# First weight tile of w1 behind w2, and the parts of Strassen's chunk, begun at other places modulo 256 bytes

## The chip, the cores and the metric

The kernel runs on one core of a Trainium2 chip. Its work lies on five engines with queues of their own: TensorE (PE in the profile, with its weight loads as PEld), VectorE (DVE), ScalarE (ACT), GpSimd (POOL) and SyncE (SP), which here issues the loads from memory. The metric is the time of one execution on the device in microseconds. Two executions of the kernel before took 2197.57 and 2195.24 us, median 2196.4 us.

## The reference

A model of two layers on 256 tokens of 2048 numbers, all in float32: stick-breaking attention, a perceptron, native sparse attention, a perceptron. What the change touches is the perceptron, which runs once per layer:

```python
def sqrelu_mlp(h, w1, w2):
    return jnp.square(jax.nn.relu(h @ w1)) @ w2      # w1: 2048 x 8192, w2: 8192 x 2048

def reference(x, ...):
    h = x
    for layer in range(DEPTH):                       # DEPTH = 2
        ...                                          # h = h + attention(rms_norm(h, ...))
        h = h + sqrelu_mlp(rms_norm(h, mlp_norm_g[layer]), mlp_w1[layer], mlp_w2[layer])
    return h
```

## The kernel before

**Precision.** Every product is made of three: each operand is split into a high part that TensorE's fast float32 form (fp32r) holds exactly and a low part that is the rest, and hi·hi, hi·lo and lo·hi are added up in PSUM. `split` (L129 to L136) makes the parts of a weight chunk: ScalarE writes `hi` (L133), VectorE writes `lo` (L135).

**Chunks.** Weights come in chunks of 512 KB, a tile of 128 partitions by 1024 numbers (4 KB a partition), and each chunk is worked off by one of three functions:

- `chunk_T` (L177) is for w1 (and for q and k). The weight chunk is TensorE's stationary operand, and x (`xs`, high and low) streams past it, 256 columns at a time. A chunk is 24 matmuls (L185): 16 with `hi`, then 8 with `lo`. Every matmul loads other weights.
- `chunk_N` (L151) is for w2 and others. The activations `yhi`, `ylo` are stationary, and the weight chunk streams, 512 columns at a time: 8 matmuls with `hi`, then 4 with `lo` (L155).
- `chunk_S` (L211) is for a quarter of w2: Strassen's seven products in place of eight. The activations (`yhi`, `ylo`, and their sums `ss`) are stationary. What streams, 256 columns at a time, are four tiles: `shi` and `slo` (three quarters of the chunk itself; L221 to L227) and `thi` and `tlo` (four sums of quarters, from `split`, L228). Seven products of three matmuls are 21 matmuls a chunk (L246): 6 stream `shi`, 3 stream `slo`, 8 stream `thi`, 4 stream `tlo`.

**The order of the work.** A perceptron (`mlp`, L390) is done in four groups, `fg` 0 to 3. In each, `group1` (L400) makes 2048 of the 8192 hidden numbers: four calls of `proj_T` (one for each `fb`), each eight chunks of w1, so 32 chunks or 768 matmuls in a row. Then `group2` (L426) takes these through w2: 24 chunks with `chunk_N`, and 8 with `chunk_S` spread among them by a short rule (L430 to L434). So with two perceptrons there are eight groups, 64 calls of `chunk_S`, and six stretches of w1 that directly follow matmuls of w2 (`fg` 1 to 3 of either layer). The stretch of `fg` 0 follows the attention's output projection, and transposes of h stand between its first chunks (L303, from `make_x`). Engines are kept in step by semaphores that the framework sets; their order is that of the code.

**Places.** The tiles `hi` and `lo` of `split`, `shi` and `slo` are 64 numbers (256 bytes) longer than what they hold, and what they hold begins at an offset, in numbers of 4 bytes:

```python
PAD = 64
NEAR, FAR, SUM = 0, 16, 48
```

`chunk_N` uses NEAR (0 bytes), `chunk_T` FAR (64 bytes), `chunk_S` SUM (192 bytes) for all four parts. In the built program the tiles `xs`, `yhi`, `ylo`, `ss`, `shi`, `slo` and every buffer of `hi` and `lo` begin at the same place modulo 256 bytes, and each matmul's slice of them lies a multiple of 256 bytes further on, so the offset alone says how the stationary and the streaming operand of a matmul lie to each other modulo 256 bytes: equal in `chunk_N`, stationary 64 bytes further in `chunk_T`, streaming 192 bytes further in `chunk_S`, which modulo 256 is again stationary 64 bytes further.

Of the kernel before, what the change touches and what calls it, by code (L numbers as in the profile page):

```python
# [9 lines left out]
F32R = mybir.dt.float32r  # L10
# [5 lines left out]
P = 128  # L16
T = 256
NT = T // P
D = 2048
KD = D // P  # L20
NB = 512
# [4 lines left out]
KC = 2  # L26
# [13 lines left out]
def hybrid_kernel(  # L40
# [13 lines left out]
    wsum = None  # L54
# [63 lines left out]
    def drain():  # L118
        while beside:
            for _ in beside.pop(0)[0]:  # L120
                pass

    PAD = 64
    NEAR, FAR, SUM = 0, 16, 48

    def split(raw, o=(NEAR, NEAR)):  # L129
        n = KC * NB  # L130
# [46 lines left out]
    def chunk_T(ps, src, k0, n0, first, last, nk=KC, o=None):  # L177

        nm = KC * NB // P // nk
        hi, lo = src if isinstance(src, tuple) else load_split(src, k0, nk, n0, nm * P, o=o or (FAR, FAR))  # L180
        tiles = [(kk, m) for kk in range(nk) for m in range(nm)]

        def mm(w, x, kk, m, s, e):
            o = ps[m // 2][:, (m % 2) * T:(m % 2 + 1) * T]
            nc.tensor.matmul(o, w[:, kk, m * P:(m + 1) * P], x[:, k0 + kk, :], start=s, stop=e, skip_group_check=True)  # L185

        for kk, m in tiles:
            mm(hi, xhi, kk, m, first and kk == 0 and m % 2 == 0, False)
            mm(hi, xlo, kk, m, False, False)
        pump()  # L190
        for kk, m in tiles:
            mm(lo, xhi, kk, m, False, last and kk == nk - 1)
        pump()

    def proj_T(ps, src, n0, nk=KC, o=None):
        for k0 in range(0, KD, nk):
            chunk_T(ps, src, k0, n0, k0 == 0, k0 + nk == KD, nk, o)

    def proj_Th(src, n0):

# [10 lines left out]
    def chunk_S(ps, src, k0, n0, first, last, ahi, alo, shi, slo, koff=0):  # L211


        W = NB // 2
        raw = load(src, k0, KC, n0, NB)
        flat = raw.rearrange("p k n -> p (k n)")

        ts = wsum.tile([P, 4, W], F32, tag="ts", name="ts")
        b12 = flat[:, 3 * W:].unsqueeze(1).to_broadcast([P, 2, W])
        nc.vector.tensor_tensor(ts[:, :2, :], flat[:, W:3 * W].rearrange("p (a n) -> p a n", a=2), b12, op=OP.subtract)  # L220
        hi, lo = [  # L221
            wsum.tile([P, 3 * W + PAD], F32R, tag=n, name=n, bufs=1)[:, SUM:SUM + 3 * W] for n in ("shi", "slo")
        ]
        nc.scalar.activation(hi, flat[:, :3 * W], AF.Copy)
        nc.vector.tensor_tensor(ts[:, 2, :], ts[:, 0, :], flat[:, 2 * W:3 * W], op=OP.add)
        nc.vector.tensor_tensor(ts[:, 3, :], flat[:, :W], ts[:, 2, :], op=OP.subtract)  # L226
        nc.vector.tensor_tensor(lo, flat[:, :3 * W], hi.bitcast(F32), op=OP.subtract)  # L227
        thi, tlo = split(ts, (SUM, SUM))  # L228
        k = k0 - koff
        y = lambda a, kk, t: a[:, k + kk, t * P:(t + 1) * P]  # L230
        s = lambda a, i: a[:, k // KC, i, :]
        b = lambda w, i: w[:, i * W:(i + 1) * W]
        trivial = [
            (0, y(ahi, 1, 0), y(alo, 1, 0), b(hi, 2), b(lo, 2)),
            (1, y(ahi, 0, 0), y(alo, 0, 0), b(hi, 0), b(lo, 0)),
            (2, s(shi, 3), s(slo, 3), b(hi, 1), b(lo, 1)),
        ]
        sums = [
            (6, s(shi, 2), s(slo, 2), thi[:, 0, :], tlo[:, 0, :]),
            (4, s(shi, 0), s(slo, 0), thi[:, 1, :], tlo[:, 1, :]),  # L240
            (5, s(shi, 1), s(slo, 1), thi[:, 2, :], tlo[:, 2, :]),
            (3, y(ahi, 0, 1), y(alo, 0, 1), thi[:, 3, :], tlo[:, 3, :]),
        ]

        def mm(i, a, w, s, e):
            nc.tensor.matmul(ps[i], a, w, start=s, stop=e, skip_group_check=True)  # L246

        for i, xh, xl, wh, wl in trivial + sums:

            mm(i, xh, wh, first and i in (0, 1, 6, 4), False)  # L250
            mm(i, xl, wh, False, False)
        pump()
        for i, xh, xl, wh, wl in trivial + sums:
            mm(i, xh, wl, False, last)
        pump()
# [134 lines left out]
    def mlp(l, layer, junk, done, last=None):  # L390
        w1, w2 = mlp_w1[l], mlp_w2[l]
        ss = junk.tile([P, 2, KD // 2, 4, P], F32R, name="ss", bufs=1)
        row = junk.tile([P, T], F32, name="row", bufs=1)

        def rows():
            yield
            pb = bcast_rows(make_rstd(layer))
            nc.scalar.activation(row, pb[:, :T], AF.Copy)

        def group1(fg, pools):  # L400

            for fb in range(D // NB):
                ps = [bank(*pools[fb % 2]) for _ in range(NB // P // 2)]
                proj_T(ps, w1, fg * D + fb * NB)
                k, n = fb * (NB // P), NB // P
                a = junk.tile([P, n, T], F32, tag="pre", name="pre", bufs=1)
                for j in range(0, n, 2):
                    nc.vector.scalar_tensor_tensor(
                        a[:, j:j + 2, :], ps[j // 2].rearrange("p (m t) -> p m t", m=2), 0.0,
                        row.unsqueeze(1).to_broadcast([P, 2, T]), op0=OP.max, op1=OP.mult,  # L410
                    )
                s = junk.tile([P, n, T], F32, tag="sq", name="sq", bufs=1)
                nc.scalar.activation(s, a, AF.Square)
                nc.scalar.activation(yhi[:, k:k + n, :], s, AF.Copy)
                nc.vector.tensor_tensor(ylo[:, k:k + n, :], s, yhi[:, k:k + n, :].bitcast(F32), op=OP.subtract)

                sv = s.rearrange("p (j kk) t -> p j kk t", kk=2)
                a1, a2 = [[sv[:, :, kk, t * P:(t + 1) * P] for kk in (1, 0)] for t in range(NT)]
                q = junk.tile([P, 2, 4, P], F32, tag="sums", name="sums", bufs=1)
                nc.vector.scalar_tensor_tensor(q[:, :, 0, :], a2[0], -1.0, a2[1], op0=OP.mult, op1=OP.subtract)  # L420
                nc.vector.tensor_tensor(q[:, :, 2, :], a1[0], a2[0], op=OP.subtract)
                nc.vector.tensor_tensor(q[:, :, 1, :], a2[1], q[:, :, 2, :], op=OP.subtract)
                nc.vector.tensor_tensor(q[:, :, 3, :], a1[1], q[:, :, 1, :], op=OP.subtract)
                split_evac(ss[:, 0, k // 2:k // 2 + 2], ss[:, 1, k // 2:k // 2 + 2], q)

        def group2(fg, plain, strassen, end):  # L426

            NK = KD // KC
            order, si = [], 0
            for i in range(3 * NK):  # L430
                order.append(((0, 1, 3)[i // NK], i % NK))
                if si < NK and i >= (3 + 1.75 * si if end else 4 + 2.25 * si):
                    order.append((2, si))
                    si += 1  # L434
            for nb, i in order:
                k0 = fg * KD + i * KC
                args = (w2, k0, nb * NB, i == 0, i == NK - 1, yhi, ylo)
                if nb == 2:
                    if i == 0:
                        bs, s = banks_S(*strassen)  # L440
                    chunk_S(s, *args, ss[:, 0], ss[:, 1], koff=fg * KD)
                    if i == NK - 1:
                        add_S(nb, bs, s, junk)
                        if end:
                            for n in range(3):
                                done(n, strassen)
                    continue
                if i == 0:
                    ps = [bank(*plain) for _ in range(NT)]
                out = last is not None and end and nb == 3  # L450
                chunk_N(ps, w2, k0, nb * NB, i == 0, i == NK - (2 if out else 1), yhi, ylo, koff=fg * KD,
                        by_token=out and i == NK - 1)
                if i == NK - 1:
                    if out:
                        add_out(nb, ps, last)
                        return
                    add_h(nb, ps)
                    if end and nb == 3:
                        done(nb, plain)

        spawn(rows(), 1)
        A, B = (acc, "acc"), (att, "att")
        for fg in range(DFF // D):
            end = fg == DFF // D - 1
            group1(fg, ((A, B), (B, A))[fg % 2])
            group2(fg, *((A, B), (B, A))[fg % 2], end)
# [200 lines left out]
    with tc.tile_pool(name="m0p", bufs=2) as mp:  # L667
        wsum = mp
# [9 lines left out]
    with tc.tile_pool(name="nsa", bufs=2) as ap, ExitStack() as last:  # L678
# [255 lines left out]
        for i in range(2):  # L934
            cT = cp.tile([P, G, T], F32, tag="cT", name="cT", bufs=1)
            for b in range(2):
                ps = proj_Th(w_in, C0 + i * NB + b * T)
# [61 lines left out]
        for g in range(G):  # L999
            ps = [bank(acc, "acc") for _ in range(NT)]  # L1000
# [16 lines left out]
            ps = proj_N(w_in, g * NB)  # L1017
# [8 lines left out]
    with tc.tile_pool(name="m1p", bufs=2) as mp:  # L1026
        wsum = mp
# [36 lines left out]
```

## Time and profile before

| | |
|---|---|
| median of 2 runs | 2196.4 us (2195.24 to 2197.57) |
| the profiled execution, its time | 2196.84 us |
| its span from first to last instruction | 2195.1 us |
| granted clock of TensorE | 0.999 |
| TensorE busy | 2186.2 us, 14482 matmuls |
| weight loads busy | 1997.6 us |
| VectorE, ScalarE, GpSimd busy | 1484.1, 1164.7, 42.5 us |
| matmuls of w1 and the like (L185) | 8040 |
| matmuls of Strassen's chunks (L246) | 1344 |

The profile is of one execution, taken by the hardware profiler. It says of each engine how long it was busy, what it waited for, and in the timeline when each group of like instructions began. A matmul's length in it is modelled and overlaps that of the next, so the pace of a row of matmuls is read from starts: the start of the next row less that of this one, over the count.

### The profile page before, as it was taken

The page shows a single profiled execution, that of the slowest core. Times are in us where ns is not written, and L with a number is a line of the kernel's source. Part 1 is how long each engine was busy: PE and PEld are TensorE (multiplying, and loading weights), DVE is VectorE, ACT ScalarE, POOL GpSimd, SP SyncE. Part 2 cuts the span into 40 slices and gives each one's busy share as a digit, 9 for nine tenths or more (in the row PEclk, how much of TensorE's full clock was granted, in tenths as well). Part 3 has the DMA queues.
Part 4 walks back from the last instruction along what each step waited for, and adds up shares of the span by engine and source line. Part 5 has one row for each costly group of instructions (what it writes and reads, how often), then busy time and mean ns, then how long its engine had stood idle before and what let it go on. Part 6 is the DMA issues. An engine that isn't in the chain of part 4 may idle for free.

```text
span 2195.1 us, 36040 instructions
## 1 busy us (share of the span) xinstructions
PE 2186.2 (100%) x14482; PEld 1997.6 (91%) x14482; DVE 1484.1 (68%) x1968; ACT 1164.7 (53%) x1537; POOL 42.5 (2%) x75
## 2 busy tenths in 40 slices
PE   9999999999999999999999999999999999999999
PEld 9999988998998998899898888889989989989998
DVE  4655556677667667767777877755776676677676
ACT  5555565455445454445546666655544454554453
POOL 0000000000000000000000011000000000000000
PEclk9999999999999999999999999999999999999999
DMA  6655555665665765665667554456657656656654
GB/s 222 204 180 172 156 182 176 186 197 186 200 190 175 215 187 178 215 185 184 203 182 222 163 144 139 139 164 186 190 189 206 182 192 202 191 183 205 189 186 160
DMA packets 260784, 406.28 MB, mean 185 GB/s; under 512 B 13188, under 2 KB 91912, under 8 KB 260616
## 3 DMA queue, kind: packets, MB, share of 16 engines
q1 hardware_dynamic: 259800, 403.52, 60.0%
q8 instruction: 113, 1.85, 0.3%
q10 hardware_dynamic: 816, 0.46, 0.1%
q14 instruction: 55, 0.45, 0.1%
HBM read 401.83 MB, written 2.10 MB: 184 GB/s over the span
## 4 chain that ended last, share of the span: by engine, by line
PE 99%; DVE 0%; POOL 0%; ACT 0%; issue 0%; DVEq 0%; ACTq 0%; POOLq 0%
PE acc L155 31%; PE acc L185 26%; PE att L185 16%; PE att L155 13%; PE acc L246 4%; PE att L246 4%; PE att L896 1%; PE att L303 1%; PE att L888 0%; PE att L889 0%; PE att L890 0%; PE att L583 0%; PE att L631 0%; PE att L842 0%; PE att L844 0%; PE att L843 0%
## 5 line engine op out<-in xcount | busy, mean ns | idle before, releaser
L133 ACT ACTIVATE hi<-raw 128x1024 fp32r<-128x1024 f32 x687 | 726.5, 1059 | 740.3 <-PE acc L155 227.1
L135 DVE TENSOR_TENSOR lo<-raw,hi 128x1024 fp32r<-128x1024 f32 x687 | 836.0, 1221 | 395.6 <-ACT hi L133 374.7
L185 PE MATMUL acc<-xs,hi 128*128 128x256 f32 x3312 | 420.4, 280 | 1.9 <-ACT hi L133 1.9
L185 PEld LDWEIGHTS acc<-xs,hi 128*128 128x128 f32 x3312 | 400.1, 189 | 2.7 <-ACT hi L133 2.1
L185 PE MATMUL att<-xs,hi 128*128 128x256 f32 x2048 | 259.8, 280 | 0.0
L155 PE MATMUL acc<-hi,yhi 128*128 128x512 f32 x640 | 250.7, 392 | 0.0
L155 PE MATMUL acc<-hi,ylo 128*128 128x512 f32 x640 | 249.3, 390 | 0.0
L185 PEld LDWEIGHTS att<-xs,hi 128*128 128x128 f32 x2048 | 248.3, 189 | 0.3
L185 PE MATMUL acc<-xs,lo 128*128 128x256 f32 x1656 | 226.5, 279 | 0.0
L185 PEld LDWEIGHTS acc<-xs,lo 128*128 128x128 f32 x1656 | 207.4, 189 | 0.0
L155 PE MATMUL acc<-hi,xs 128*128 128x512 f32 x704 | 177.2, 392 | 0.0
L155 PE MATMUL acc<-lo,yhi 128*128 128x512 f32 x640 | 172.4, 390 | 0.0
L155 PEld LDWEIGHTS acc<-hi,xs 128*128 128x128 f32 x704 | 130.3, 188 | 26.6
L155 PE MATMUL att<-hi,yhi 128*128 128x512 f32 x380 | 148.2, 390 | 0.0
L155 PE MATMUL att<-hi,ylo 128*128 128x512 f32 x380 | 147.9, 389 | 0.0
L155 PEld LDWEIGHTS acc<-lo,yhi 128*128 128x128 f32 x640 | 119.5, 188 | 24.9 <-issue 0.4
L155 PEld LDWEIGHTS acc<-hi,ylo 128*128 128x128 f32 x640 | 120.2, 188 | 23.3 <-DVE ylo L290 0.2
L155 PEld LDWEIGHTS acc<-hi,yhi 128*128 128x128 f32 x640 | 120.2, 188 | 23.3 <-ACT yhi L289 0.2
L185 PE MATMUL att<-xs,lo 128*128 128x256 f32 x1024 | 140.4, 280 | 0.0
L185 PEld LDWEIGHTS att<-xs,lo 128*128 128x128 f32 x1024 | 128.7, 189 | 0.0
L220 DVE TENSOR_TENSOR ts<-raw 128x512 f32<-128x512 f32 x64 | 44.3, 692 | 115.6 <-DMA raw<-in_mlp_w_dram 115.5
L133 ACT ACTIVATE hi<-ts 128x1024 fp32r<-128x1024 f32 x64 | 67.8, 1059 | 87.8 <-DVE ts L226 41.8
(290 smaller groups left out, 2501.3 us busy)
## 6 DMA issues: line engine op xcount, KB each, us to landing
raw<-in_mlp_w_dram SPq DMA_DIRECT2D x512, 512.0 KB, 3.9
raw<-in_sb_w_qkv_dram SPq DMA_DIRECT2D x95, 512.0 KB, 3.8
raw<-in_nsa_w_in_dram SPq DMA_DIRECT2D x50, 512.0 KB, 3.8
raw<-in_sb_w_out_dram SPq DMA_DIRECT2D x32, 512.0 KB, 3.9
raw<-in_nsa_w_in_dram SPq DMA_DIRECT2D x64, 256.0 KB, 3.4
raw<-in_nsa_w_out_dram SPq DMA_DIRECT2D x32, 512.0 KB, 3.7
w1t<-in_nsa_cmp_w_dram SPq DMA_DIRECT2D x8, 512.0 KB, 4.9
h<-in_x_dram SPq DMA_DIRECT2D x8, 256.0 KB, 4.1
```

Source lines behind the costliest of these rows:

```text
L133: nc.scalar.activation(hi, raw, AF.Copy)
L135: nc.vector.tensor_tensor(lo, raw, hi.bitcast(F32), op=OP.subtract)
L155: mm = lambda a, b, k, t, s, e: nc.tensor.matmul(ps[t], a[:, k, t * P:(t + 1) * P], b, start=s, stop=e)
L185: nc.tensor.matmul(o, w[:, kk, m * P:(m + 1) * P], x[:, k0 + kk, :], start=s, stop=e, skip_group_check=True)
L220: nc.vector.tensor_tensor(ts[:, :2, :], flat[:, W:3 * W].rearrange("p (a n) -> p a n", a=2), b12, op=OP.subtract)
L246: nc.tensor.matmul(ps[i], a, w, start=s, stop=e, skip_group_check=True)
L303: nc.tensor.transpose(ps[:, j * T + t * P:j * T + (t + 1) * P], h[:, t, (kp + j) * P:(kp + j + 1) * P], ident)
L896: nc.tensor.transpose(ptp[:w, j * P:(j + 1) * P], src(j), ident)
```

## The change

Only places change. The first chunk of w1 of `fg` 1, 2 and 3 in either layer (`fb` 0, `k0` 0) begins 32 bytes into its tiles (`TURN`) where it began 64 bytes in; the other 31 chunks of the stretch stay at 64. In `chunk_S` a counter of the calls picks, for each of the eight groups, another set of four offsets, for `shi` (A), `slo` (B), `thi` (C) and `tlo` (E). In bytes, where all were 192:

| group | shi | slo | thi | tlo | matmuls of a chunk's 21 that stream from another place |
|---|---|---|---|---|---|
| layer 0, fg 0 | 224 | 192 | 192 | 192 | 6 |
| layer 0, fg 1 | 224 | 192 | 192 | 224 | 10 |
| layer 0, fg 2 | 224 | 224 | 192 | 192 | 9 |
| layer 0, fg 3 | 32 | 192 | 192 | 192 | 6 |
| layer 1, fg 0 | 192 | 192 | 224 | 192 | 8 |
| layer 1, fg 1 | 240 | 192 | 192 | 192 | 6 |
| layer 1, fg 2 | 128 | 192 | 192 | 192 | 6 |
| layer 1, fg 3 | 192 | 224 | 192 | 224 | 7 |

No tile changes its size or its place in memory. No instruction is added, taken out or moved: on every engine the two programs have the same instructions in the same order, with the same shapes and waits. Of the matmuls, 144 load their weights from another place (six chunks of 24), and 464 stream from another place (58 in the table, times eight chunks in a group).

```diff
     PAD = 64
-    NEAR, FAR, SUM = 0, 16, 48
+    NEAR, FAR, TURN, SUM = 0, 16, 8, 48
...
-    def proj_T(ps, src, n0, nk=KC, o=None):
+    def proj_T(ps, src, n0, nk=KC, turn=False):
         for k0 in range(0, KD, nk):
-            chunk_T(ps, src, k0, n0, k0 == 0, k0 + nk == KD, nk, o)
+            o = TURN if turn and k0 == 0 else FAR
+            chunk_T(ps, src, k0, n0, k0 == 0, k0 + nk == KD, nk, (o, o))
...
+        A, B, C, E = ((56, 48, 48, 48), (56, 48, 48, 56), (56, 56, 48, 48), (8, 48, 48, 48), (48, 48, 56, 48),
+                      (60, 48, 48, 48), (32, 48, 48, 48), (48, 56, 48, 56))[trial[0] // 8]
+        trial[0] += 1
         hi, lo = [
-            wsum.tile([P, 3 * W + PAD], F32R, tag=n, name=n, bufs=1)[:, SUM:SUM + 3 * W] for n in ("shi", "slo")
+            wsum.tile([P, 3 * W + PAD], F32R, tag=n, name=n, bufs=1)[:, o:o + 3 * W]
+            for n, o in (("shi", A), ("slo", B))
         ]
...
-        thi, tlo = split(ts, (SUM, SUM))
+        thi, tlo = split(ts, (C, E))
...
-                proj_T(ps, w1, fg * D + fb * NB)
+                proj_T(ps, w1, fg * D + fb * NB, turn=fg > 0 and fb == 0)
```

## Rows read from the trace of the kernel before

**Rows 1.** The page: the span, each engine's busy time, and the chain of work that ended last by engine.

```profile
span 2195.1 us, 36040 instructions
PE 2186.2 (100%) x14482; PEld 1997.6 (91%) x14482; DVE 1484.1 (68%) x1968; ACT 1164.7 (53%) x1537; POOL 42.5 (2%) x75
...
PE 99%; DVE 0%; POOL 0%; ACT 0%; issue 0%; DVEq 0%; ACTq 0%; POOLq 0%
```

**Rows 2.** All waits of TensorE for another engine over the whole span: us in total, times, longest.

```profile
PE acc L185 <- ACT hi L133: 1.9, 1, 1.9
PE att L489 <- POOL ident masks.py:199: 1.6, 1, 1.6
PE att L761 <- DVE hs L757: 0.9, 1, 0.9
PE att L796 <- DVE kc L792: 0.5, 1, 0.5
PE acc L508 <- ACT hi L501: 0.2, 1, 0.2
```

**Rows 3.** Busy time by stretch, of the matmuls of L185 alone. The stretches are w1's of `fg` 0 (first and fifth row, from the second chunk behind the last transposes on) and of `fg` 1 to 3 (the others, whole), layer 0 and then layer 1. Columns: stretch, its length, TensorE busy and count, weight loads busy and count, granted clock, share of the DMA engines busy, GB/s.

```profile
415.79:486.51 70.72, 70.72 (x626) 70.68 (x624) 1.00 0.66 193
571.60:662.05 90.45, 90.45 (x768) 90.41 (x767) 1.00 0.65 190
747.15:837.60 90.45, 90.45 (x768) 90.41 (x767) 1.00 0.65 190
922.69:1013.15 90.46, 90.46 (x768) 90.41 (x767) 1.00 0.64 187
1508.51:1579.23 70.72, 70.72 (x626) 70.69 (x624) 1.00 0.65 194
1664.33:1754.78 90.45, 90.45 (x768) 90.41 (x767) 1.00 0.66 190
1839.87:1930.32 90.45, 90.45 (x768) 90.41 (x767) 1.00 0.65 190
2015.42:2105.87 90.45, 90.45 (x768) 90.41 (x767) 1.00 0.65 189
```

**Rows 4.** TensorE's timeline at the last transposes ahead of w1 of `fg` 0, layer 0: start, length in us, engine, line, operands, count.

```profile
412.82 0.38 PE L352 MATMUL att<-ident,rstd 128*128 128x128 f32 x2
412.96 2.09 PE L185 MATMUL acc<-xs,hi 128*128 128x256 f32 x16
414.88 1.07 PE L185 MATMUL acc<-xs,lo 128*128 128x256 f32 x8
415.79 1.98 PE L185 MATMUL acc<-xs,hi 128*128 128x256 f32 x16
```

**Rows 5.** TensorE's timeline at the step from w2 of `fg` 0 to w1 of `fg` 1, layer 0; columns as in rows 4.

```profile
568.88 0.39 PE L155 MATMUL acc<-hi,yhi 128*128 128x512 f32 x1
...
570.69 1.07 PE L155 MATMUL acc<-lo,yhi 128*128 128x512 f32 x4
571.60 2.05 PE L185 MATMUL att<-xs,hi 128*128 128x256 f32 x16
573.48 1.11 PE L185 MATMUL att<-xs,lo 128*128 128x256 f32 x8
574.43 2.05 PE L185 MATMUL att<-xs,hi 128*128 128x256 f32 x16
```

**Rows 6.** TensorE's timeline from the first matmul of Strassen's first chunk (500.13) to the first behind it (502.61), and over the two chunks of `chunk_N` that follow.

```profile
500.13 0.28 PE L246 MATMUL att<-shi,yhi 128*128 128x256 f32 x1
...
502.49 0.28 PE L246 MATMUL att<-lo,yhi 128*128 128x256 f32 x1
502.61 0.39 PE L155 MATMUL acc<-hi,yhi 128*128 128x512 f32 x1
...
505.33 0.39 PE L155 MATMUL acc<-hi,yhi 128*128 128x512 f32 x1
...
508.05 0.39 PE L155 MATMUL acc<-hi,yhi 128*128 128x512 f32 x1
```

**Rows 7.** The costliest groups of the page: how many chunks go through `chunk_S` (L220 is its first instruction on VectorE), and ScalarE's writing of `hi` with its idle time.

```profile
L133 ACT ACTIVATE hi<-raw 128x1024 fp32r<-128x1024 f32 x687 | 726.5, 1059 | 740.3 <-PE acc L155 227.1
...
L220 DVE TENSOR_TENSOR ts<-raw 128x512 f32<-128x512 f32 x64 | 44.3, 692 | 115.6 <-DMA raw<-in_mlp_w_dram 115.5
```

**Rows 8.** TensorE's timeline in native sparse attention's compression, where L750 runs 32 matmuls of 256 columns whose stationary operand (120 columns) begins 224 bytes further, modulo 256, from one matmul to the next.

```profile
1199.17 3.94 PE L750 MATMUL att<-ws,bs 128*120 128x256 f32 x32
1202.95 1.32 PE L155 MATMUL acc<-hi,xs 128*128 128x512 f32 x5
```

**Rows 9.** TensorE's timeline at the step from w1 to w2 of `fg` 1, layer 0: the first two chunks of `chunk_N`.

```profile
662.05 0.40 PE L155 MATMUL att<-hi,yhi 128*128 128x512 f32 x1
662.29 0.40 PE L155 MATMUL att<-hi,ylo 128*128 128x512 f32 x1
662.52 0.39 PE L155 MATMUL att<-hi,yhi 128*128 128x512 f32 x1
...
664.80 0.39 PE L155 MATMUL att<-hi,yhi 128*128 128x512 f32 x1
...
666.61 1.07 PE L155 MATMUL att<-lo,yhi 128*128 128x512 f32 x4
```

More of the change, by code (lines that the diff above doesn't have):

```diff
@@ L121, in drain @@
                 pass
+    trial = [0]
     PAD = 64
-    NEAR, FAR, SUM = 0, 16, 48
+    NEAR, FAR, TURN, SUM = 0, 16, 8, 48
     def split(raw, o=(NEAR, NEAR)):
```

## The prediction

> **What bounds the kernel now.** I read the page first. TensorE is busy for 2186.2 of 2195.1 us, and the chain of work that ended last is TensorE's own for 99% [rows 1]. The view of its waits shows five waits, 5.1 us together; the rest of the span is matmuls one behind the other [rows 2]. So time comes and goes only through the pace at which matmuls follow each other, and the next view to read is the pace by stretch. It shows something odd. The 624 matmuls of w1 of `fg` 0 take 70.72 us, 113.33 ns each; the 768 of each later stretch take 90.45 us, 117.77 ns each. That is the same instruction with the same shape, the same offsets and the same granted clock of 1.00 (2.4 GHz), beside as many bytes a second. Each pace holds from one end of its stretch to the other, through every change of chunk and bank, in both layers [rows 3]. It is not starvation: with a wait for an operand the profile would show TensorE idle, and there is none here. So there are two steady states, and which one holds is settled where the stretch begins.
>
> The timelines show how they begin. In `fg` 0 a pair of transposes breaks the stream, the 24 matmuls behind it take 2.83 us (117.9 ns each), and from the next chunk on the fast pace holds [rows 4, 3]. In `fg` 1 to 3 w1 follows `chunk_N`, whose twelve matmuls take 2.72 us, 226.7 ns each, which is twice 113.33; there w1 starts without a break, at 2.83 us a chunk at once, and stays so [rows 5, 3]. Strassen's chunk, too, follows `chunk_N` without a break: 2.48 us for 21 matmuls, 118 ns each, and `chunk_N` behind it is back at 2.72 us with its first chunk [rows 6]. I take from this that a stream of weights and a stream of moving data step through memory in a fixed rhythm to each other, that the fast rhythm and the slow one both keep themselves up, and that a break or a shift can move one into the other. That is an inference; the rows show only the two paces and where they begin.
>
> **The change part by part.** No instruction comes or goes, so the sum holds paces only. It is made against the profiled execution's 2196.8 us (its span is 2195.1); the median, 2196.4, is 0.4 less.
>
> *The turned chunk of w1.* Six chunks load their weights 32 bytes earlier. What matters is whether the shift in and the shift back leave the rest of the stretch in the slow rhythm or in the fast one. The trace of before has no such shift, so the two bounds are the two paces. If it stays slow, the gain is nothing. If it turns, 744 matmuls behind the first chunk gain 4.44 ns in each of six stretches: 6 x 744 x 4.44 = 19.8 us. For the turned chunk itself I take the price of the settling chunk of `fg` 0, 2.83 us [rows 4], what such a chunk costs now [rows 5], so it is worth nothing. The shift back costs at most what a step between kinds of matmul costs, 0.03 us: `chunk_N` behind w1 takes 2.75 us in place of 2.72 before it is in pace [rows 9, 6]. Six of them are 0.2 us. Nothing else has to speed up: `fg` 0 runs at the fast pace with no wait of TensorE, at 193 GB/s against 187 to 190 [rows 2, 3], and ScalarE, which writes `hi`, has 740 us of idle time ahead of those very instructions [rows 7]; were that cover gone, TensorE would wait for `hi` and the 19.8 us would shrink. I take 19.6 us of gain, since the fast rhythm, once there, outlives everything in its stretch, and one break sufficed to find it; against it stands that all six starts from `chunk_N` go wrong in one and the same way.
>
> *Strassen's parts.* 64 chunks [rows 7] of 21 matmuls, of which 464 stream from another place. Below, the bound is the fast pace for all 1344: (118 - 113.33) x 1344 = 6.3 us of gain. Above, the dearest pace that the rows show outside a break is `chunk_N`'s first two matmuls behind w1, 0.47 us for the two [rows 9] against 0.453 in pace, 8 ns more each: 1344 x 8 = 10.8 us, and 0.03 us at each of the 128 ends, 3.8 us; together 14.6 us of loss. The nearest row is L750's: the same width, with the stationary operand's place running through eight different ones modulo 256 bytes, 3.78 us for 32 matmuls, 118.1 ns each [rows 8]. So a matmul at any of these places costs on average what Strassen's cost now, and I take nothing for the matmuls themselves. But today's chunk hands the stream back in pace, and one at other places has no reason to: 64 x 0.03 = 1.9 us of loss, which I take. Writing to other places costs nothing that counts, since ScalarE and VectorE are 53% and 68% busy [rows 1].
>
> The sum: 2196.8 - 19.6 + 1.9 = 2179.1, so 2179 us.
>
> **The rivals.**
>
> *The shift does nothing to w1.* The slow rhythm may simply follow the weights by 32 bytes and back. For it speaks that it survives 31 changes of chunk in each stretch [rows 3], each of which could have upset it, and that L750's matmuls at ever other places average 118.1 ns, the slow pace and not the fast one [rows 8]. Against it: none of those changes of chunk moves the place modulo 256 bytes, and this one does. Time: 2196.8 + 1.9 = 2198.7 us.
>
> The Trainium skill has a rule that would end in the same place. "TensorE: Matmul & The Clock Gate", section "Step-by-step: what each phase is for", gives TensorE two independent read ports into SBUF, one for the moving operand and one for weight loads, and "SBUF — State Buffer", section "SBUF: two separate sides", says that TensorE never waits on anyone there. By that rule the place of an operand would be worth nothing anywhere, Strassen's parts included, and the time would stay at 2196.8 us. The two paces of one and the same instruction in this trace [rows 3] do not fit it well, but they do not show a place at work either.
>
> *Only some of the stretches turn.* Each stretch follows another layout of Strassen's chunk, so the six need not begin alike. Against it: `chunk_N` finds its pace within a chunk [rows 9] and runs several chunks before w1 begins. With three of six, 2196.8 - 9.8 + 1.9 = 2189 us.
>
> *Strassen's chunks fall out of step (slower).* The four parts now lie at different places within one chunk, so the stream is shifted several times in 21 matmuls and may never settle. Place: L246 and the first `chunk_N` behind it. Price: the upper bound, 14.6 us. For it speaks that 192 bytes for all parts gives seamless steps at both ends [rows 6], which is more than w1's end can say [rows 9]. Against it speaks L750's average [rows 8]. With w1 turned it could not win, as it would have to lose 19.6 / 64 = 0.31 us a chunk and its bound is 0.23; with w1 as it is, any loss makes the kernel slower. Full price with w1 unturned: 2211 us.
>
> **How the numbers follow.** The turn works in all six: 0.48. It does nothing: 0.37. It works in some: 0.08. Strassen's chunks lose well over 1.9 us with w1 unturned: 0.07. The first is the likeliest, so I predict 2179 us, with a range of its own from 2171 (Strassen's matmuls at the fast pace as well: 2196.8 - 19.6 - 6.3) to 2185 (four times the loss that I take for Strassen's parts). It is hardly likelier than the second, so the range must hold that too: from 2171 to 2203, the second with Strassen's loss at some three times my price. That leaves out most of the last rival and a few hundredths at the ends of the others.
>
> A change of 2%, about what a measurement of this kernel can tell from no change, is 44 us. No bound reaches it: the largest gain is 19.8 + 6.3 = 26 us, the largest loss 14.6 and whatever six stretches of w1 could lose in a still slower rhythm, which no row shows. So faster by over 2% gets 0.01, slower by over 2% 0.01, and within 2% 0.98.
>
> **What would show it.** The pace by stretch is the first view to read: in the six stretches of `fg` 1 to 3, 113.3 ns (about 87.1 us a stretch) if the turn works, 117.8 (90.45) if not, and something between or above in some of them otherwise. The timeline of the first two chunks tells whether the pace changes in the turned chunk or at the shift back. For Strassen's parts, the length of a chunk of L246 against 2.48 us and of the `chunk_N` behind it against 2.72 us, group by group; the groups differ in which parts lie elsewhere, and should differ in time if places matter at all. `fg` 0's w1 should be untouched. I am wrong in the mechanism, and not only in its luck, if the six stretches keep 117.8 ns to the digit and all eight layouts of Strassen's chunk keep 2.48 us: then places modulo 256 bytes do nothing, and the two paces come from something else.

## The result, and the profile after

The changed kernel takes 2177.46 us, the median of two executions (2176.14 and 2178.78), against 2196.4 us before: a ratio of 0.9911, 95% interval 0.9887 to 0.9934. I had said 2179, in a range of 2171 to 2203. The profiled execution took 2176.14 us, with a span of 2174.4.

In the page of the changed kernel only TensorE is different: it is busy 21.3 us less with the same 14482 matmuls, and its weight loads 22.6 us less. The other engines' busy times are within 0.6 us of what they were [rows 1].

```profile
span 2174.4 us, 36040 instructions
PE 2164.9 (100%) x14482; PEld 1975.0 (91%) x14482; DVE 1483.5 (68%) x1968; ACT 1165.0 (54%) x1537; POOL 42.5 (2%) x75
```

Next is the pace by stretch, as in [rows 3]; w1's matmuls are line L188 now. The first row is `fg` 0 of layer 0 (from 24 matmuls earlier than there), the second is `fg` 1 of layer 0. The other five changed stretches read the same to 0.01 us.

```profile
411.23:484.78 73.55, 73.55 (x649) 73.51 (x648) 1.00 0.66 193
570.25:657.41 87.16, 87.16 (x768) 87.12 (x767) 1.00 0.67 197
```

All six stretches went from 90.45 to 87.16 us, 3.29 us each, 19.7 together. The clock is 1.00 as before. TensorE's timeline at the start of the first of them shows where the pace changes:

```profile
570.25 2.06 PE L188 MATMUL att<-xs,hi 128*128 128x256 f32 x16
572.15 1.11 PE L188 MATMUL att<-xs,lo 128*128 128x256 f32 x8
573.09 1.98 PE L188 MATMUL att<-xs,hi 128*128 128x256 f32 x16
...
575.81 1.41 PE L188 MATMUL att<-xs,hi 128*128 128x256 f32 x11
```

The turned chunk itself takes 2.84 us (570.25 to 573.09), no less than the first chunk did before [rows 5]. The chunk behind it, back at 64 bytes, takes 2.72 us at once, 113.3 ns a matmul, and so do all that follow.

w2 by group, all of TensorE's work from the first `chunk_N` to the next w1. Here are three groups of before (`fg` 0 and 3 of layer 0, `fg` 3 of layer 1; the other five are at 85.09 or 85.10 too):

```profile
486.51:571.60 85.09, 85.09 (x458) 1.00 0.61 195
...
1013.15:1083.74 70.59, 70.59 (x394) 1.00 0.59 199
...
2105.87:2188.24 82.37, 82.37 (x446) 1.00 0.53 180
```

and the eight of the changed kernel, in order:

```profile
484.78:570.25 85.47, 85.47 (x458) 1.00 0.61 194
657.41:742.78 85.37, 85.37 (x458) 1.00 0.60 194
829.94:915.09 85.15, 85.15 (x458) 1.00 0.60 195
1002.25:1073.16 70.91, 70.91 (x394) 1.00 0.61 203
1568.70:1653.97 85.27, 85.27 (x459) 1.00 0.59 195
1741.12:1825.85 84.73, 84.73 (x458) 1.00 0.59 194
1913.01:1997.90 84.89, 84.89 (x459) 1.00 0.59 195
2085.06:2167.54 82.48, 82.48 (x447) 1.00 0.54 182
```

Six layouts cost 0.06 to 0.38 us a group, two gain (0.36 with `shi` at 240 bytes, 0.20 with it at 128). Their sum is 0.75 us of loss. How that comes about is seen in the timelines of a chunk: first a group that lost (`shi` and `tlo` at 224), then the one that gained most (`shi` at 240). The rows are the first matmul of Strassen's chunk (L254 now), the first behind it, and the first of the next chunk.

```profile
671.04 0.28 PE L254 MATMUL acc<-shi,yhi 128*128 128x256 f32 x1
...
673.52 0.40 PE L158 MATMUL att<-hi,yhi 128*128 128x512 f32 x1
...
676.27 0.39 PE L158 MATMUL att<-hi,yhi 128*128 128x512 f32 x1
```

```profile
1754.75 0.28 PE L254 MATMUL acc<-shi,yhi 128*128 128x256 f32 x1
...
1757.16 0.39 PE L158 MATMUL att<-hi,yhi 128*128 128x512 f32 x1
...
1759.90 0.39 PE L158 MATMUL att<-hi,yhi 128*128 128x512 f32 x1
```

In the first, Strassen's chunk is as long as before (2.48 us) and `chunk_N` behind it takes 2.75 in place of 2.72 us [rows 6]. In the second the chunk takes 2.41 us, and `chunk_N` behind it 2.74: 0.06 to 0.07 gained, 0.02 given back. Read so in all eight groups, the 64 chunks of Strassen's are 0.7 us shorter together than before, and the 64 chunks of `chunk_N` behind them 1.4 us longer.

What is left of the span's 20.7 us is at the start: the first matmul of L188 begins at 10.11 us, where in the trace of before it (L185) begins at 11.75. No place that the change moves is in use that early, and over the traces here that start lies anywhere between 9.66 and 11.82 us. 19.7 - 0.75 + 1.64 = 20.6 us.

### The profile page after: what moved, and what is told of

The parts are those of the page before. It is cut to its first block, busy times and chain, and to the rows that moved or that the text cites. A ratio compares the mean times of both kernels' runs of the same rounds, so it can differ in the third digit from the quotient of the medians.

```text
span 2174.4 us, 36040 instructions
## 1 busy us (share of the span) xinstructions
PE 2164.9 (100%) x14482; PEld 1975.0 (91%) x14482; DVE 1483.5 (68%) x1968; ACT 1165.0 (54%) x1537; POOL 42.5 (2%) x75
## 4 chain that ended last, share of the span: by engine, by line
PE 99%; DVE 0%; POOL 0%; ACT 0%; issue 0%; DVEq 0%; ACTq 0%; POOLq 0%
PE acc L158 31%; PE acc L188 26%; PE att L188 16%; PE att L158 13%; PE att L254 4%; PE acc L254 4%; PE att L904 1%; PE att L311 1%; PE att L896 0%; PE att L897 0%; PE att L898 0%; PE att L591 0%; PE att L639 0%; PE att L850 0%; PE att L852 0%; PE att L851 0%
## 5 line engine op out<-in xcount | busy, mean ns | idle before, releaser
L188 PE MATMUL acc<-xs,hi 128*128 128x256 f32 x3312 | 413.8, 278 | 1.9 <-ACT hi L136 1.9
L188 PEld LDWEIGHTS acc<-xs,hi 128*128 128x128 f32 x3312 | 394.0, 188 | 2.7 <-ACT hi L136 2.1
L188 PE MATMUL att<-xs,hi 128*128 128x256 f32 x2048 | 253.2, 276 | 0.0
L188 PEld LDWEIGHTS att<-xs,hi 128*128 128x128 f32 x2048 | 242.2, 188 | 0.3
L188 PE MATMUL acc<-xs,lo 128*128 128x256 f32 x1656 | 222.9, 277 | 0.0
L188 PEld LDWEIGHTS acc<-xs,lo 128*128 128x128 f32 x1656 | 204.2, 188 | 0.0
L188 PE MATMUL att<-xs,lo 128*128 128x256 f32 x1024 | 137.0, 276 | 0.0
L188 PEld LDWEIGHTS att<-xs,lo 128*128 128x128 f32 x1024 | 125.7, 188 | 0.0
```

## The experiments

Three theories stood at the start. By the **place theory** (the "shift theory" of the first two expectations), weights and moving data go through memory in a rhythm to each other that their places modulo 256 bytes and the moment of entry settle; the turned chunk moves w1 out of a slow rhythm into a fast one. Its rivals were that Strassen's parts had done it, by handing over to `chunk_N` in another rhythm, and that any disturbance, of whatever kind, wakes the fast pace.

**The turned chunk alone.**

```diff
-        A, B, C, E = ((56, 48, 48, 48), (56, 48, 48, 56), ...)[trial[0] // 8]
+        A, B, C, E = (SUM, SUM, SUM, SUM)
```

> The changed kernel with Strassen's four parts back at 192 bytes in all groups; the turned chunk of w1 stays. The shift theory (the turned chunk alone sets w1's rhythm): the six stretches of w1 stay at 87.16 us each, Strassen's chunk is back at 2.473 us and chunk_N behind it at 2.720 us, w2 takes 85.09 us per group again (70.59 and 82.37 in the two that end otherwise); the time is 0.8 us below the changed kernel's, some 2176 to 2177 us. The parts theory (rival: the other places of Strassen's parts change the rhythm in which chunk_N hands over, and that turns w1): the six stretches are back at 90.45 us and the time at about 2196 us.

Measured: 2176.55 us, ratio 0.9925 (0.9901 to 0.9950). All six stretches of w1 and five of the eight groups of w2 are as the shift theory has them; the first stretch is shown. In the other three groups one or two of Strassen's chunks are longer, by 0.25 to 1.8 us a group; the view of waits puts 1.3 us of that down to TensorE waiting for `slo`.

```profile
569.78:656.94 87.16, 1.00 0.68 197
```

The turned chunk does all of w1's gain. The 0.8 us that Strassen's old places should have saved do not show in the time, in which the executions differ by more (2174.7 to 2184.72 us).

**Strassen's parts alone.**

```diff
-                proj_T(ps, w1, fg * D + fb * NB, turn=fg > 0 and fb == 0)
+                proj_T(ps, w1, fg * D + fb * NB, turn=False)
```

> The changed kernel without the turned chunk: w1 begins at 64 bytes everywhere, Strassen's parts lie in eight ways. The shift theory: all six stretches of w1 at 90.45 us, the eight groups of w2 as in the changed kernel (85.47, 85.37, 85.16, 70.91, 85.26, 84.73, 84.89, 82.48 us), so 0.8 us above before: about 2197 us. The parts theory: some or all six stretches at 87.2 us, and a time towards 2177 us.

Measured: 2195.91 us, ratio 1.0005 (0.9996 to 1.0015). All six stretches of w1 are back at 90.45 us, one of them here; the groups of w2 are the changed kernel's where Strassen's chunk does not wait (85.47, 85.36, 84.72 us for the first, second and sixth). The theory that the parts had turned w1 falls.

```profile
570.52:660.97 90.45, 90.45 (x768) 90.41 (x767) 1.00 0.65 190
```

**Six other places for the first chunk.**

```diff
+    turns = [0, 4, 24, 32, 48, 56]
...
-            o = TURN if turn and k0 == 0 else FAR
+            o = FAR if turn is None or k0 else turn
...
+                proj_T(..., turn=turns.pop(0) if fg > 0 and fb == 0 else None)
```

> Strassen's parts at 192 bytes; the first chunk of the six stretches of w1 begins at 0, 16, 96, 128, 192 and 224 bytes, one each, where the changed kernel has 32, and the rest of each stretch at 64. If any shift breaks the slow rhythm, all six take about 87.2 us (113.3 ns from the second chunk on). If only some places land in the fast rhythm (a matter of the phase in which the first chunk ends), a part of the six stays at 90.4 us; by the trace of the changed kernel, where the turned chunk runs irregularly at 118.2 ns and the next is fast from its first matmul on, I expect three to five of six to turn, and a time between 2177 and 2187 us.

Measured: 2180.63 us. The six stretches, first chunk at 0, 16, 96, 128, 192 and 224 bytes:

```profile
567.90:658.40 90.50, 90.50 (x768) 90.45 (x767) 1.00 0.65 190
743.49:833.96 90.47, 90.47 (x768) 90.42 (x767) 1.00 0.65 192
919.05:1006.20 87.15, 87.15 (x768) 87.11 (x767) 1.00 0.66 192
1657.36:1744.57 87.21, 87.21 (x768) 87.17 (x767) 1.00 0.68 197
1829.66:1916.82 87.16, 87.16 (x768) 87.12 (x767) 1.00 0.67 197
2001.92:2089.04 87.12, 87.11 (x768) 87.08 (x767) 1.00 0.65 193
```

Four turn, two do not. With the changed kernel's 32 that makes five places of seven, the six new ones tried in one stretch each. So a shift as such is not enough, and 32 bytes are nothing special.

**A disturbance in time, with every place as before.** The first matmul of each of the six stretches is done as two of 128 columns.

```diff
+            if cut and kk == m == 0:
+                for c in (slice(0, P), slice(P, T)):
+                    nc.tensor.matmul(ps[0][:, c], hi[:, 0, :P], xhi[:, k0, c], start=c.start == 0, stop=False,
+                                     skip_group_check=True)
+            else:
                 mm(hi, xhi, kk, m, first and kk == 0 and m % 2 == 0, False)
```

> No place differs from before: w1 at 64 bytes throughout, Strassen's parts at 192. In the six stretches only the first matmul is cut into two of 128 columns, which disturbs the stream in time alone. The place theory (the pace hangs on where weights and moving data lie to each other, and on the phase in which a stretch is entered; a disturbance in time can shift the phase, too, but need not): the six act alike, since all six begin in the same phase, so all at 87.2 us or all at 90.45. The rival, that any disturbance wakes the fast pace: all six at 87.2 us and a time of about 2176 us. All six at 90.45 us (about 2196 us) would show that a disturbance as such is not enough.

Measured: 2178.01 us. All six stretches turn; the timeline of the first, and the same stretch as a whole (with the two short matmuls):

```profile
571.66 0.34 PE L193 MATMUL att<-xs,hi 128*128 128x128 f32 x2
571.83 1.94 PE L188 MATMUL att<-xs,hi 128*128 128x256 f32 x15
573.61 1.07 PE L188 MATMUL att<-xs,lo 128*128 128x256 f32 x8
574.51 1.75 PE L188 MATMUL att<-xs,hi 128*128 128x256 f32 x14
```

```profile
571.66:658.83 87.17, 87.17 (x770) 1.00 0.67 197
```

The two short ones take 0.17 us, the 15 behind them 1.78 us (118.7 ns each, still settling), the 8 after that 0.90 us (113 ns): the fast pace holds before the first chunk is over. No place was moved, though the cut adds one matmul and one weight load to each stretch. So the two paces are two states of one and the same arrangement, and the change of place in the changed kernel was only one way to get from one into the other. By itself this result fits the rival, that any disturbance will do, as well.

**One place for the whole stretch.**

```diff
+    turns = [0, 8, 32, 48, 56, 60]
...
-            o = TURN if turn and k0 == 0 else FAR
+            o = FAR if turn is None else turn
...
+                proj_T(..., turn=(None, *turns)[fg + 3 * (layer == 'm1')] if fg else None)
```

> Strassen's parts at 192 bytes. In the six stretches of w1 all 32 chunks lie at one place, with no shift inside the stretch: 0, 32, 128, 192, 224 and 240 bytes in turn. Place theory: each place has its own steady pace from this start, and the stretch at 32 bytes keeps the irregular 118.2 ns that the turned chunk had in the changed kernel (90.8 us), since the shift back is what turned it. If the shift back is not needed, the stretch at 32 falls to 113.3 ns (87.1 us) by itself. For the others I expect between 113.3 and 118.5 ns: 87 to 91 us.

Measured: 2199.82 us. The stretches at 0, 32, 128, 192, 224 and 240 bytes:

```profile
569.88:662.03 92.15, 92.15 (x768) 92.10 (x767) 1.00 0.63 186
747.14:838.01 90.87, 90.87 (x768) 90.83 (x767) 1.00 0.64 189
923.13:1015.30 92.17, 92.17 (x768) 92.11 (x767) 1.00 0.64 183
1668.51:1758.96 90.45, 90.45 (x768) 90.40 (x767) 1.00 0.65 190
1844.04:1933.64 89.60, 89.60 (x768) 89.56 (x767) 1.00 0.65 192
2018.73:2108.84 90.11, 90.11 (x768) 90.06 (x767) 1.00 0.64 189
```

At 32 bytes the stretch stays at 118.3 ns (90.87 / 768), so in the changed kernel it was the step back to 64 that brought the fast pace. The others lie between 116.7 and 120.0 ns; the two at 120.0 are above what I had allowed. None finds 113.3 from this entry. So the place matters by itself, too: the same instructions differ by up to 2.6 us a stretch by it. Whether each place has one pace only is not shown, as each was tried in one stretch and from one entry, and 64 bytes have two.

**Other layouts of Strassen's parts.**

```diff
-        A, B, C, E = ((56, 48, 48, 48), (56, 48, 48, 56), ...)[trial[0] // 8]
+        A, B, C, E = ((60, 60, 48, 48), (60, 60, 60, 60), (60, 48, 60, 48), (48, 60, 48, 48), (48, 48, 60, 48),
+                      (48, 48, 48, 60), (52, 48, 48, 48), (4, 48, 48, 48))[trial[0] // 8]
```

> The changed kernel with eight other layouts of Strassen's parts around its best one, shi, slo, thi, tlo in bytes: 240 240 192 192; 240 240 240 240; 240 192 240 192; 192 240 192 192; 192 192 240 192; 192 192 192 240; 208 192 192 192; 16 192 192 192. Place theory: w1 unmoved at 87.16 us in all six; each group has its own length of Strassen's chunk between 2.38 us (113.3 ns a matmul) and 2.53, the same for all eight chunks of a group; chunk_N behind it between 2.720 and 2.765 us. One layout in which all four parts share a place (240) hands over in its own way but has no shift inside; if shifts inside the chunk cost, it is among the shortest. The time is within 5 us of the changed kernel's.

Measured: 2176.34 us. w1 stays at 87.16 us in all six. No group is better than with `shi` alone at 240 bytes (84.73): the first two, `shi` and `slo` at 240 and all four at 240, are

```profile
483.34:568.22 84.88, 84.88 (x458) 1.00 0.60 196
655.38:740.94 85.56, 85.56 (x459) 1.00 0.59 194
```

so all four at 240 bytes, with no shift inside the chunk, is not among the best. Of its 0.47 us above before, 0.2 is one chunk that takes 2.69 us where its seven like take 2.46; the rest is lost at the step to `chunk_N` (2.76 us). The guess that shifts inside the chunk are what costs is wrong: `shi` alone at 240 has them, and its chunk takes 2.41 us.

**Other places for `chunk_N`.** w2's `chunk_N` streams its weights from 16, 32, 64, 96, 128, 192, 224 and 240 bytes in the eight groups, everywhere else 0; the turned chunk is in.

```diff
+    near = [4, 8, 16, 24, 32, 48, 56, 60]
...
-        hi, lo = src if isinstance(src, tuple) else load_split(src, k0, KC, n0, NB)
+        hi, lo = src if isinstance(src, tuple) else load_split(src, k0, KC, n0, NB, o=(o, o))
...
+                        by_token=out and i == NK - 1, o=near[fg + 4 * (layer == 'm1')])
```

> Strassen's parts at 192 bytes and the turned chunk as in the changed kernel; chunk_N of w2, which streams its weights from 0 bytes in all kernels so far, streams them from 16, 32, 64, 96, 128, 192, 224 and 240 bytes in the eight groups. Place theory: chunk_N, too, has a pace of its own at each place, at or above the 226.7 ns at 0 bytes; no better one shows unless twice 113.3 ns is not the floor. w1 behind it is entered in other phases, so some of the six stretches lose their turn (90.4 us) though their first chunk is shifted as before. If only the relation of the two operands counts, chunk_N at 64 more should be as Strassen's stream at 64 more relative to its weights; a pace below 226 ns in any group would be a gain of some microseconds in a better kernel.

Measured: 2198.3 us. Every group is dearer than at 0 bytes, by 0.7 to 1.9 us (85.82 us at 64 bytes, 86.99 at 224); `chunk_N` in its steady pace takes from 2.75 us (64 bytes) to 2.84 (240) in place of 2.72. More telling are the six stretches of w1 behind them, all with the same turned chunk, behind `chunk_N` at 16, 32, 64, 128, 192 and 224 bytes:

```profile
569.83:660.29 90.46, 90.46 (x768) 90.42 (x767) 1.00 0.64 189
746.54:833.72 87.18, 87.17 (x768) 87.13 (x767) 1.00 0.66 196
919.54:1010.00 90.46, 90.46 (x768) 90.42 (x767) 1.00 0.64 186
1663.33:1750.51 87.18, 87.18 (x768) 87.13 (x767) 1.00 0.67 196
1837.43:1927.90 90.47, 90.47 (x768) 90.42 (x767) 1.00 0.64 188
2014.89:2105.35 90.46, 90.46 (x768) 90.42 (x767) 1.00 0.64 186
```

Four of six lose the turn. The same shift leads to the fast or to the slow pace by what stands ahead of it. That speaks against the rival that any disturbance wakes the fast pace, as the first chunk at 0 and 16 bytes does, and for a state that is carried over from one matmul to the next.

Strassen's chunks say the same in this trace. Their parts lie at 192 bytes in all groups, but behind `chunk_N` at 32, 96 and 128 bytes all but the first of a group take 2.38 to 2.39 us, 113.3 to 113.7 ns a matmul; behind 16, 64, 192 and 224 bytes they stay at 2.47. Here is one behind 32 bytes (its first matmul and the first behind it):

```profile
685.09 0.28 PE L254 MATMUL acc<-shi,yhi 128*128 128x256 f32 x1
...
687.47 0.39 PE L159 MATMUL att<-hi,yhi 128*128 128x512 f32 x1
```

So they, too, have a slow and a fast pace at one place, and what runs ahead picks between them.

**The shift met a second time, from the fast pace.**

```diff
-                proj_T(ps, w1, fg * D + fb * NB, turn=fg > 0 and fb == 0)
+                proj_T(ps, w1, fg * D + fb * NB, turn=fg > 0 and fb in (0, 2))
```

> Strassen's parts at 192 bytes; in the six stretches the first chunk is shifted to 32 bytes and back, and the 17th (the first of fb 2) again, now from within the fast pace. If a shift out and back always leads to the fast pace, each stretch stays at about 87.3 us (one chunk more at 118.2 ns costs 0.1). If it is a matter of the phase in which the shift is met, it can throw the second half back to 117.8 ns: about 88.9 us a stretch and 2187 us; all six act alike in either case.

Measured: 2180.27 us; Strassen's parts are at 192 bytes here. All six stretches take 87.28 us, 0.12 more: one chunk at 118.2 ns, and the fast pace again behind it. The time is not the stretches' doing: the last group of w2 takes 86.14 us in place of 82.37, with one wait of 1.9 us for `slo` and a granted clock of 0.98 over the group.

```profile
570.18:657.46 87.28, 87.28 (x770) 1.00 0.67 197
```

From this entry, too, 32 bytes and back lead to the fast pace. Together with the four stretches before, "always" is still not so.

**The best layout in all groups.**

```diff
-        A, B, C, E = ((56, 48, 48, 48), (56, 48, 48, 56), ...)[trial[0] // 8]
+        A, B, C, E = (60, SUM, SUM, SUM)
```

> The changed kernel with the layout of its best group in all eight: shi at 240 bytes, the other three parts at 192; the turned chunk stays. If a group's time is that of its layout alone, Strassen's chunk takes 2.412 us and chunk_N behind it 2.735 us in every group, w2 takes 84.73 us (0.36 less than before; 70.2 and 82.0 in the two that end otherwise), and the time is some 3.6 us below the changed kernel's: about 2173 to 2174 us. If the gain of that one group came from what stood ahead of it, the other groups differ.

Measured: 2170.64 us once, and every group of w2 at the length of the one in the changed kernel, so a group's time is that of its layout:

```profile
483.02:567.75 84.73, 84.73 (x458) 1.00 0.59 196
```

The same kernel once more, timed:

> The same kernel as the one with shi at 240 bytes in all groups and the turned chunk, now timed: its one time so far was 2170.6 us. If the six stretches (19.8 us) and eight groups (2.9 us) add up, it is 22.6 us below the kernel before: about 2173 us, ratio 0.990, and 3.6 us below the changed kernel.

Measured: 2174.45 us (2172.2 to 2177.24), ratio to the kernel before 0.9901 (0.9885 to 0.9918). That is 3.0 us below the changed kernel's median, about the 3.6 that the groups give, but by the times alone the two kernels cannot be told apart. In this trace TensorE waits for `slo` in two places, 0.8 us together, which the trace before it did not show; such waits of Strassen's chunk for its parts appear in several of the kernels here, with w1 turned or not, up to 1.9 us, and none in the traces of before and of the changed kernel.

## Why the prediction was right

**What bounds the kernel.** Right: but for the 1.64 us of the earlier start, the gain came through TensorE's pace, and no engine had to become faster for it. TensorE waits nowhere new in the changed kernel's trace. The start is luck of the two profiled executions, and no term of the sum stands for it; the two medians differ by 18.9 us, which is about the 19.7 of w1 less the 0.75 of w2.

**The turned chunk.** Right in every part of the term: 19.6 us forecast, 19.7 measured. The settling chunk was priced at 2.83 us and took 2.84. The shift back was priced at 0.03 us at most and cost nothing. It is the step that I gave 0.48, and that it went this way was in part luck: of seven places for the first chunk two leave w1 slow, and behind other places of `chunk_N` the same shift fails in four stretches of six. That all six begin alike, which I held against it, was what made it all or nothing.

**Strassen's parts.** 1.9 us of loss forecast, 0.75 measured. Both halves of that step were off, and both made the loss too large. "I take nothing for the matmuls themselves" missed two groups, whose chunks became shorter (2.41 us against 2.47 with `shi` at 240 bytes); over all groups the chunks gained 0.7 us. The hand-over cost 1.4 us and not 1.9: that a chunk at other places "has no reason to" hand back in pace was too strict, for behind `shi` and `slo` at 224 bytes `chunk_N` is in pace at once (2.72 us), and elsewhere it costs between 0.01 and 0.05 us.

**The inference of a rhythm.** It was drawn from two paces and their beginnings, and the experiments bear it out as far as they go: the fast pace can be reached with no place moved (the cut matmul), the pace changes with the place (the whole stretches), and the outcome of a shift hangs on what ran ahead of it (`chunk_N` moved). What in the memory makes the rhythm, and why 0 and 16 bytes fail where 32 to 224 succeed, stays open; no experiment here looked at a single access.

One reading under it was incomplete. The transposes of [rows 4] did not bring `fg` 0 into the fast pace, which held ahead of them already. The trace of before shows the turn a little earlier: the chunk ahead of the first transposes takes 2.83 us (400.92 to 403.75), and the one ahead of those in [rows 4] 2.72 (410.10 to 412.82).

```profile
400.92 2.05 PE L185 MATMUL acc<-xs,hi 128*128 128x256 f32 x16
...
403.75 0.60 PE L303 MATMUL att<-ident,h 128*128 128x128 f32 x4
...
410.10 1.98 PE L185 MATMUL acc<-xs,hi 128*128 128x256 f32 x16
```

So `fg` 0 begins slow, as the other stretches do, and transposes between its chunks bring the fast pace; those of [rows 4] interrupt it for 16 matmuls. That one break can suffice is right all the same: behind the first four transposes the eight `lo` matmuls are already at some 114 ns.

**The rivals.** "The shift does nothing" was refuted by the turned chunk alone. The rule of the Trainium skill, in "TensorE: Matmul & The Clock Gate", section "Step-by-step: what each phase is for", that moving data and weight loads have independent read ports, does not lead to the right time here if it is taken to mean that places are worth nothing: with the same instructions and only the place of the weights changed, a stretch takes 89.60 to 92.17 us. Whether the ports themselves are independent no run here shows. "Only some turn" is what other places gave, not this one. Strassen's chunks did not fall out of step: the worst layout, in a group with no wait and no single long chunk, cost 0.38 us (85.47 against 85.09), 0.05 us a chunk, where the bound was 0.23.

## What to carry to other kernels

Where TensorE is busy all the time, compare the pace of the same instruction between stretches: two steady paces at one clock and no waits mean that something other than work sets it, here 4.4 ns a matmul over 4608 matmuls. Look at what stands directly ahead of the slow stretch, and try to disturb its first matmul or to move its first operand by a few dozen bytes, since the state, once reached, lasts for hundreds of matmuls. Not every shift does it: two of seven places failed here, and the one that worked failed behind four of six other places of `chunk_N`. Sweep it stretch by stretch in one kernel, and read each from the trace: differences of 0.1 us a stretch are plain there and invisible in the time.

## What I had not expected of the hardware

A stretch of 768 matmuls keeps either of two paces, 113.3 and 117.8 ns, with every address, clock and neighbour the same, and two matmuls of 128 columns in place of one of 256, 0.17 us, decide which. With the weights of the whole stretch at other places modulo 256 bytes its pace was from 116.7 to 120.0 ns at the six tried. And the pace of 512 columns at equal places, 226.7 ns, is the best of nine tried: at all others `chunk_N` took 2.75 to 2.84 us in place of 2.72.
